# Weights in 2 MB transfers into pairs of pieces: a two-layer hybrid with two mixture-of-experts stages

## The chip, the cores and the metric

The kernel runs on one core of one Trainium2 chip (trn2). A core has TensorE (PE), VectorE (DVE), ScalarE (ACT), GpSimd (POOL) and SyncE (SP), which only issues transfers here, and 16 DMA engines. The metric is the time of one execution on the device in microseconds (us), the median of several. Memory of the chip is called HBM, the working memory of a core has 128 partitions.

## The reference

Two layers over x of 256 tokens x 1024 features, in fp32:

```
u = rms_norm(h); h = h + mixer(u); u = rms_norm(h); h = h + moe(u)

mixer of layer 0: proj = u @ w_in (1024 x 3592), split into seven parts of 512 and one of 8;
    a gated recurrence over chunks (8 heads of 64), and causal attention with a forget gate
    (8 heads of 64); both joined, @ w_out (1024 x 1024)
mixer of layer 1: q, k, v = u @ w_in (1024 x 3072); q, k normalised by head, their gains, rope;
    8 heads, each softmax(q1 k1) - lam * softmax(q2 k2), times v; normalised, @ w_out
moe: 4 groups of 8 experts; each token takes the best group, and its best 2 experts in it;
    for g: y += (silu(x @ w_gate[g]) * (x @ w_up[g]) * combine) @ w_down[g]
    w_gate, w_up: 1024 x 512 and w_down: 512 x 1024 for each of 32 experts
```

The weights of one expert are three matrices of 2 MB (1 MB here is 1024 KB), 192 MB a layer; the mixers have 17 matrices of 2 MB. All of it is read once: 418 MB in 1 MB pieces of 128 partitions x 2048 numbers.

## The kernel before

**Stages.** Mixer 0, experts of layer 0, mixer 1, experts of layer 1. In a mixer the tokens' features are turned by PE and split into two float parts (`transposed`), each weight piece is split too into a high and a low part (`Weights.ahead`: ACT copies at L294, DVE subtracts at L295), and each product is three matmuls (`mm3`, L269 to L271). In an expert stage the tokens are sorted to experts, up to 32 tokens (CAP) an expert, eight rounds (`qd`) of four experts (`es`). An expert takes 16 products with gate and up (L1254, two matmuls each on the chip), SiLU and product on ACT and DVE, 16 products with down (L1264). The first expert's products with gate and up stand apart (`first_products`, L1199), so do the last expert's (`products` L1295, `down` L1306), whose results are scattered back to the tokens (L1226) and added to h (L1232).

**The ring.** `Slots` is a ring `R` of 22 slots of 1 MB (128 x 2048 numbers). It is both the place where weight pieces land and the place of the mixers' work buffers: `alloc` and `hold` give a slot to the program, `free(n, keep)` gives slots back, of which `keep` stay reserved for later buffers, and `want(n)` keeps back the next ones given free. Whatever is not live and not reserved is filled by `pump` with the next piece in the order of use: one transfer of 1 MB (L102), 8192 contiguous bytes a partition. The split weights take slots too, `SPLIT` of them at a time, one for each half of a piece.

**What sets the order.** The transfers stand in one queue, issued by SP in program order. Each one waits for its slot (the last engine that used it), and on one of eight semaphore lanes (DMAHW0 to 7 in the order), that is for the landing of the transfer eight before it; a transfer that waits holds up all behind it. The order of work on the engines is made by a scheduler from the program's order, the data and the free tiles, with some edges written by hand (`issue_after`). PE's products of the projections are spread by it between the heads' steps: scores (L375), turning probabilities (L402), applying them (L410 to L414), turning a head's result (L861).

**Other transfers** on the queue: x, constants, `wrt` (the router's weights of a layer, 160 KB, L214; the second layer's go out after the last reader of the first's, L999 on PE) and the output.

Of the kernel before, what the change touches and what calls it, by code (L numbers as in the profile page):

```python
# [29 lines left out]
SLOTS = 22  # L30
SPLIT = (5, 5)
KEPT = 5 + SPLIT[0], 3 + SPLIT[1]

# [11 lines left out]
V_FQ, V_FK, V_DQ, V_DK, V_N = 70, 71, 72, 136, 200  # L45
# [14 lines left out]
class Slots:  # L60


    def __init__(self, nc, pool, chunks, n, reserve):
        self.nc, self.pool, self.chunks, self.n = nc, pool, chunks, n
        self.live, self.reserve, self.due = 0, reserve, 0
        self.issued, self.taken = [], 0

    def tile(self, dt=F32):
        return self.pool.tile([P, 2048], dt, name="w", tag="w", bufs=self.n)

    def alloc(self, dt=F32):
        assert self.reserve > 0
        self.reserve -= 1
        self.live += 1
        return self.tile(dt)

    def hold(self):

        t = self.alloc()
        self.nc.gpsimd.memset(t[:, 0:1], 0.0)  # L80
        return t

    def halves(self):
        t = self.hold()
        return t[:, 0:1024], t[:, 1024:2048]
# [11 lines left out]

    def pump(self, most=1000):
        while most > 0 and self.live + self.reserve < self.n and len(self.issued) < len(self.chunks):
            src, k = self.chunks[len(self.issued)]  # L100
            w = self.tile().rearrange("p (k f) -> p k f", k=k)
            self.nc.sync.dma_start(out=w, in_=src)  # L102
            self.issued.append(w)
            self.live += 1
            most -= 1

    def take(self):
        self.taken += 1
        return self.issued[self.taken - 1]

# [12 lines left out]
def hybrid_kernel(ctx: ExitStack, tc: tile.TileContext, x, pos, vec, wr, wbf, const,  # L123
# [4 lines left out]
    ring = ctx.enter_context(tc.tile_pool(name="ring", bufs=SLOTS))  # L128
# [38 lines left out]
    wbh = cst.tile([P, 2, KD, 8], F32R, name="wbh")  # L167
# [16 lines left out]
    def pieces(w, ks):  # L184

        return [(w[i].rearrange("p (k f) -> p k f", k=k), k) for i, k in enumerate(ks)]
# [16 lines left out]
    chunks = pieces(w_mix0, KS0) + experts(0) + pieces(w_mix1, KS1) + experts(1)  # L203
    R = Slots(nc, ring, chunks, SLOTS, KEPT[0])
    R.pump(2)
    nc.sync.dma_start(out=ct[:, C_N0:C_N], in_=const[:, C_N0:C_N])
    nc.sync.dma_start(out=wbt, in_=wbf)
    R.pump(2)
# [17 lines left out]
    def transposed(gain, W=None):  # L226

        uh, ul = (R.alloc(F32R).rearrange("p (k s) -> p k s", k=KD) for _ in range(2))

# [43 lines left out]
    class Weights:  # L273


        def __init__(self, n, slots):
            self.n, self.free = n, slots
            self.ready, self.rest = [], []

        def ahead(self, most=1000):  # L280
            while self.n > 0 and self.free > 0 and most > 0:
                most -= 1
                self.n -= 1
                self.free -= 1
                last = len(self.rest) == 1
                if not last:
                    w = R.take()
                    k = w.shape[1]
                    self.rest = [w[:, :, i * P:i * P + P] if k == KD else w[:, i * k // 2:(i + 1) * k // 2, :]
                                 for i in range(2)]  # L290
                w = self.rest.pop(0)
                t = R.alloc(F32R)
                hi, lo = (t[:, 1024 * i:1024 * i + 1024].rearrange("p (k f) -> p k f", k=w.shape[1]) for i in range(2))
                self.split = A.copy(out=hi, in_=w)  # L294
                V.tensor_tensor(out=lo, in0=w, in1=hi.bitcast(F32), op=ALU.subtract)  # L295
                if last:
                    R.free(1)
# [6 lines left out]
        def done(self):  # L304
            self.free += 1
            R.free(1, keep=1 if self.n > 0 else 0)
# [109 lines left out]
    def maps():  # L416


        x = [R.hold() for _ in range(2)]
        Ls = [[x[1][:, 384 * (2 * i + j):384 * (2 * i + j) + 384] for j in range(2)] for i in range(2)]  # L420
        Ls.append([w[:, 1536:1920] for w in x])
        return pairs(x[0]), Ls
# [4 lines left out]
    def split_halves():  # L427

        a = R.alloc(F32R)
        return tuple(a[:, 1024 * i:1024 * i + 1024].rearrange("p (m t) -> p m t", m=4) for i in range(2))  # L430

    class OutProj:
# [18 lines left out]
        def first(self, o):  # L451
            for k in range(4):
                self.block(o, k, k == 0)
            R.free(1)
# [20 lines left out]
    def even():  # L475
        v4 = lambda a: a.rearrange("p (m t) -> p m t", m=4)
        uT, ia, iv = transposed(vt[:, V_GM:V_GM + 8])
        W = Weights(36, SPLIT[0])
# [26 lines left out]
        f_, B_ = R.halves()  # L505
        f, B = v4(f_), v4(B_)
        q2_ = R.hold()
        Az_ = R.hold()
# [7 lines left out]
        R.want(3)  # L516
# [52 lines left out]
        Ts, g_ = R.halves()  # L569
        ST0_, ST1_ = R.halves()  # L570
        STh = [v4(a) for a in (ST0_, ST1_)]
        S1_, va_ = R.halves()
# [73 lines left out]
        R.free(1)  # L646
# [81 lines left out]
        o = []  # L728
        R.want(1)
        R.free(2)  # L730
        values()
        qk = [v4(a) for a in R.halves()]
# [3 lines left out]
        R.want(1)  # L736
        first_out(3)
        R.free(1)
        first_out(1)
        heads_in(qk[1], vt[:, V_FK:V_FK + 1])  # L740
        R.want(1)
        PT, Ls = maps()
        R.free(1)
        R.want(1)
        R.free(1)
        R.want(1)
        o.append(split_halves())
        softmax(0, qk, Ls[0], PT[0])
        PT += pairs(R.hold())
        softmax(1, qk, Ls[1], PT[1])  # L750
        gates(0, *o[0])
        R.want(1)
        softmax(2, qk, Ls[2], PT[2])
        gates(1, *o[0])
        R.free(2)
        softmax(3, qk, Ls[0], PT[3])
        o.append(split_halves())
# [9 lines left out]
        R.free(2)  # L767
        second_out(3, PT[3], *o[1])
        R.free(1, keep=1)
# [4 lines left out]
    def rope_tables():  # L774
# [18 lines left out]
        for i, (off, scale) in enumerate(((V_DQ, 0.125), (V_DK, 1.0))):  # L793
            gv = vt[:, off:off + 64].rearrange("p (a b) -> p a b", a=2).unsqueeze(1).broadcast_to([P, NT, 2, 32])
            for j, tr in enumerate((cos, sin)):
                dst = rope_t[:, 2 * i + j].rearrange("p t (a b) -> p t a b", a=2)
                G.tensor_tensor(out=dst, in0=gv, in1=tr.unsqueeze(2).broadcast_to([P, NT, 2, 32]), op=ALU.mult)
# [3 lines left out]
    def odd(W):  # L801
        uT, ia, _ = transposed(vt[:, V_GM + 8:V_GM + 16], W)
# [23 lines left out]
        qk = [[v4(a) for a in R.halves()]]  # L826
# [51 lines left out]
        o = []  # L878
        R.want(2)
        heads_in(qk[0], 0)  # L880
        qk.append([v4(a) for a in R.halves()])
        o.append(split_halves())
        R.want(1)
        heads_in(qk[0], 1)
        R.want(1)
        PT, Ls = maps()
        R.want(2)
        R.free(1)
        p0 = [soft(0, qk[0], Ls[0]), soft(1, qk[0], Ls[1])]
        heads_in(qk[1], 0)  # L890
        with tc.issue_after(W.last.ins):
            p_transposed(p0, PT[0])
        W.ahead()
        PT += pairs(R.hold())
        v = [a.rearrange("p (t c) -> p t c", t=NT) for a in R.halves()]
# [13 lines left out]
        head_out(3, v[0], PT[1], *o[0])  # L909
        R.free(1)  # L910
        head_out(2, v[0], PT[1], *o[0])
        R.want(1)
        R.free(1)
        o.append(split_halves())
# [3 lines left out]
        R.free(1)  # L918
# [3 lines left out]
        R.free(2)  # L922
        head_out(6, v[1], PT[3], *o[1])
        head_out(7, v[1], PT[3], *o[1])
        R.free(1, keep=1)
# [6 lines left out]
    def moe(l, op):  # L932
        gain = vt[:, V_GF + 8 * l:V_GF + 8 * l + 8]
        hk = h.rearrange("p t (q k) -> p t k q", k=KD)
        work = [R.alloc()]
# [252 lines left out]
        def first_products():  # L1188
# [7 lines left out]
            for n in range(2):  # L1196
                for x_ in range(2):
# [3 lines left out]
                    R.free(1)  # L1201
# [34 lines left out]
        spare = 0  # L1236
        for qd in range(8):
# [5 lines left out]
            if qd == 7 and l == 0:  # L1243
                spare = KEPT[1] - 8
            ys = buffers(qd)[1]
            for es in range(4 if qd < 7 else 3):
                if qd == 0 and es == 0:
                    hid = hidden(*gp0)
                else:
# [6 lines left out]
                    R.free(4, keep=min(spare, 4))  # L1256
                    spare -= min(spare, 4)
# [12 lines left out]
                R.free(2, keep=1 if qd == 0 and es == 0 else 0)  # L1270
# [9 lines left out]
                if es == 2 and qd == 0:  # L1280
                    work.append(R.alloc())
# [158 lines left out]
```

## Time and profile before

| what | value |
|---|---|
| median of 3 runs | 1208.14 us (1207.39 to 1208.32) |
| profiled execution: time, span | 1205.45 us, 1203.8 us |
| mean granted clock of TensorE | 0.937 |
| busy: PE, DVE, ACT, POOL | 1021.5, 351.1, 297.0, 54.1 us (85, 29, 25, 4%) |
| weights' queue | 441.44 MB, its packets 89.7% of the 16 engines' span |
| mean rate over the span | 368 GB/s |

The span is from the first to the last instruction; the execution's time has 1.65 us more around it. Busy times are sums over engines that work side by side, so what ends a stage is read from the waits in that stage, not from these shares. A packet is one contiguous run of a transfer on one DMA engine.

### The profile page before, as it was taken

What the parts mean: (1) busy time and instruction counts of PE and PEld (TensorE: products, weight loads), DVE (VectorE), ACT (ScalarE), POOL (GpSimd) and SP (SyncE); (2) the same over time, 40 slices, a digit from 0 to 9 for tenths busy, and PEclk for the clock granted to TensorE, in tenths of its full rate; (3) what the DMA queues carried; (4) which work ended last, traced back from release to release, by engine and by line L of the source; (5) the groups of instructions that cost most, each with busy time, mean ns of one, the idle gap of its engine ahead of it and who ended that gap; (6) DMA issues with size and microseconds to landing.
All of it is one profiled execution on the core that took longest, in us unless ns stands there. A gap on an engine that the chain in (4) does not pass through costs nothing.

```text
span 1203.8 us, 17689 instructions
## 1 busy us (share of the span) xinstructions
PE 1021.5 (85%) x7284; PEld 589.9 (49%) x7284; DVE 351.1 (29%) x879; ACT 297.0 (25%) x681; POOL 54.1 (4%) x100
## 2 busy tenths in 40 slices
PE   7999998898887878787788999888787868786877
PEld 7878774353433434233256778455352424252523
DVE  7877633011111101001068876311111111110101
ACT  7266532111111111101164575211111111111111
POOL 2130001000000000000002100000000000000000
PEclk8999988889989899889999999999998998998898
DMA  9741969999999999999995369799999999999996
GB/s 374 320 141 42 356 268 421 421 421 420 420 421 418 420 421 421 421 421 421 416 419 198 105 210 363 288 419 420 421 421 421 421 420 420 421 420 420 421 422 273
DMA packets 63685, 442.62 MB, mean 368 GB/s; under 512 B 7152, under 2 KB 7664, under 8 KB 10608
## 3 DMA queue, kind: packets, MB, share of 16 engines
q1 hardware_dynamic: 63600, 441.44, 89.7%
q8 instruction: 59, 0.97, 0.3%
q14 instruction: 26, 0.21, 0.0%
HBM read 440.37 MB, written 1.05 MB: 367 GB/s over the span
## 4 chain that ended last, share of the span: by engine, by line
DMA 45%; PE 18%; DVE 3%; ACT 2%; issue 1%; POOL 0%; SPq 0%; ACTq 0%; DVEq 0%; POOLq 0%
DMA w<-w_up 17%; DMA w<-w_gate 15%; DMA w<-w_down 13%; PE pa L1254 3%; PE pa L270 2%; PE pa L271 2%; PE pa L269 2%; PE pb L1077 1%; PE pa L1264 1%; PE pc L375 1%; PE pc L1226 1%; PE pb L1112 1%; PE pa L1226 1%; DVE w L295 1%; PE pb L1179 1%
## 5 line engine op out<-in xcount | busy, mean ns | idle before, releaser
L1254 PE MATMUL pa<-w 128*32 128x512 f32 x1920 | 307.3, 648 | 64.0 <-DMA w<-w_up 55.1
L1254 PEld LDWEIGHTS pa<-w 128*32 128x32 f32 x1920 | 72.1, 118 | 263.4 <-issue 140.4
L1264 PE MATMUL pa<-w,hid 128*32 128x256 f32 x1984 | 142.2, 432 | 34.6 <-DVE hid L1115 34.6
L1115 DVE TENSOR_TENSOR hid<-hid,pb 128x128 f32<-128x128 f32 x64 | 18.4, 288 | 485.8 <-ACT hid L1114 485.8
L1109 ACT COPY s<-pa 128x512 f32<-128x512 f32 x68 | 39.8, 585 | 403.7 <-PE pa L1254 360.4
L269 PE MATMUL pa<-w 128*128 128x512 f32 (+1 forms) x320 | 120.9, 379 | 3.3 <-ACT w L294 3.3
L270 PE MATMUL pa<-w 128*128 128x512 f32 (+1 forms) x320 | 118.8, 371 | 1.4 <-DVE w L295 1.4
L271 PE MATMUL pa<-w 128*128 128x512 f32 (+1 forms) x320 | 118.3, 370 | 1.8 <-DVE w L295 1.8
L1112 PEld LDWEIGHTS pb<-ct,s 128*128 128x128 f32 x544 | 66.0, 191 | 104.6 <-ACT s L1109 102.6
L1077 PE MATMUL pb<-s,h 128*128 128x128 f32 x448 | 115.8, 409 | 0.0
L1112 PE MATMUL pb<-ct,s 128*128 128x64 f32 (+1 forms) x544 | 74.2, 280 | 47.3 <-ACT s L1109 47.3
L1077 PEld LDWEIGHTS pb<-s,h 128*128 128x128 f32 x448 | 109.5, 334 | 9.3 <-issue 9.3
L1268 DVE COPY w<-pa 32x256 f32<-32x256 f32 x124 | 52.4, 423 | 179.5 <-ACT w L1268 179.1
L1264 PEld LDWEIGHTS pa<-w,hid 128*32 128x32 f32 x1984 | 63.3, 120 | 83.8 <-DVE hid L1115 41.3
L1268 ACT COPY w<-pa 32x256 f32<-32x256 f32 x124 | 44.9, 362 | 233.3 <-PE pa L1264 190.8
L295 DVE TENSOR_TENSOR w<-w 128x1024 fp32r<-128x1024 f32 x68 | 86.6, 1285 | 8.9 <-ACT w L294 8.6
L294 ACT CAST w<-w 128x1024 fp32r<-128x1024 f32 x68 | 70.0, 1046 | 22.1 <-PE pa L271 11.5
L269 PEld LDWEIGHTS pa<-w 128*128 128x128 f32 x320 | 61.7, 193 | 14.3 <-ACT w L294 4.1
L270 PEld LDWEIGHTS pa<-w 128*128 128x128 f32 x320 | 61.8, 193 | 12.4 <-issue 2.5
L271 PEld LDWEIGHTS pa<-w 128*128 128x128 f32 x320 | 61.6, 192 | 11.2 <-DVE w L295 2.1
L1096 POOL TENSOR_TENSOR s<-OH,CW 128x128 f32<-128x128 f32 x36 | 14.6, 406 | 830.8 <-PE pb L1112 518.3
L1226 PE MATMUL pc<-w,s 128*128 128x512 f32 (+1 forms) x64 | 36.7, 656 | 9.5 <-DVE w L1268 9.3
(264 smaller groups left out, 754.6 us busy)
## 6 DMA issues: line engine op xcount, KB each, us to landing
w<-w_gate SPq DMA_DIRECT2D x128, 1024.0 KB, 19.8
w<-w_up SPq DMA_DIRECT2D x128, 1024.0 KB, 19.8
w<-w_down SPq DMA_DIRECT2D x128, 1024.0 KB, 19.8
w<-w_mix SPq DMA_DIRECT2D x34, 1024.0 KB, 17.8
h<-x SPq DMA_DIRECT2D x2, 512.0 KB, 4.2
out<-h SPq DMA_DIRECT2D x4, 256.0 KB, 2.0
ct<-const SPq DMA_DIRECT2D x1, 468.0 KB, 9.8
wrt<-wr SPq DMA_DIRECT2D x2, 160.0 KB, 9.6
```

The lines of the kernel that those rows point to most:

```text
L269: T.matmul(out=out, lhsT=lhsT[0], rhs=rhs[0], start=start, stop=False)
L270: T.matmul(out=out, lhsT=lhsT[0], rhs=rhs[1], start=False, stop=False)
L271: return T.matmul(out=out, lhsT=lhsT[1], rhs=rhs[0], start=False, stop=stop)
L294: self.split = A.copy(out=hi, in_=w)
L295: V.tensor_tensor(out=lo, in0=w, in1=hi.bitcast(F32), op=ALU.subtract)
L1077: T.matmul(out=pt[:, k, :], lhsT=hk[:, t, 4 * n + k, :], rhs=og[:, t, :], start=t == 0, stop=t == NT - 1)
L1109: A.copy(out=gs, in_=g.rearrange("p (f k) -> p k f", k=4))
L1112: T.matmul(out=tp[:, k, c], lhsT=gs[:, k, :], rhs=r, start=True, stop=True)
L1226: m = T.matmul(out=y[t][:, n, :], lhsT=Sm[:, t * P:(t + 1) * P], rhs=ys, start=start, stop=stop)
L1254: T.matmul(out=gp[32 * j:32 * j + 32, :], lhsT=xg[:, 4 * (j % 2) + kk, 32 * es:32 * es + 32], rhs=w[j][:, kk, :], start=kk == 0, stop=kk = ...
L1264: m = T.matmul(out=dp[32 * j:32 * j + 32, :], lhsT=hid[:, k, :], rhs=w[k // 2][:, k % 2, 256 * j:256 * j + 256], start=k == 0, stop=k == 3 ...
L1268: (V.tensor_copy if j % 2 else A.copy)(out=ys[32 * es:32 * es + 32, 256 * j:256 * j + 256], in_=dp[32 * j:32 * j + 32, :])
```

## The change

Weights come in units of 2 MB, a whole matrix: one transfer of 16384 contiguous bytes a partition, into a tile of 128 x 4096 that holds two pieces. (The mixers' weights are laid out for that; the first two units of mixer 0 and each layer's last expert still come as two transfers of 1 MB.) The ring has 11 such pairs, room for 24 pieces with two single work buffers beside it; these two take the work buffers that need one slot. `drop(n)` counts pieces that are used up and gives a pair back when both are; split weights have three pairs, six halves, instead of five slots. `first_products` uses gate's two pieces, then up's, where it alternated. Gains of rope come by a transfer of their own (256 KB, in the middle of mixer 0) instead of within `vec`.

```diff
-SLOTS = 22
-SPLIT = (5, 5)
-KEPT = 5 + SPLIT[0], 3 + SPLIT[1]
+PAIRS = 11
+SPLIT = 3
+KEPT = 2 + SPLIT, 1 + SPLIT
+SCRATCH = 1024
...
-        return self.pool.tile([P, 2048], dt, name="w", tag="w", bufs=self.n)
+        return self.pool.tile([P, 4096], dt, name="w", tag="w", bufs=self.n)
+
+    def single(self):
+        return self.pool.tile([P, 2048], F32, name="o", tag="o", bufs=2)
...
+    def drop(self, n):
+
+        self.dropped += n
+        while self.ends and self.ends[0] <= self.dropped:
+            self.ends.pop(0)
+            self.free()
+
     def pump(self, most=1000):
-        while most > 0 and self.live + self.reserve < self.n and len(self.issued) < len(self.chunks):
-            src, k = self.chunks[len(self.issued)]
-            w = self.tile().rearrange("p (k f) -> p k f", k=k)
-            self.nc.sync.dma_start(out=w, in_=src)
-            self.issued.append(w)
+        while most > 0 and self.live + self.reserve < self.n and self.units:
+            w = self.tile()
+            a = 0
+            for src, k, n in self.units.pop(0):
+                self.nc.sync.dma_start(out=w[:, 2048 * a:2048 * (a + n)].rearrange("p (k f) -> p k f", k=k), in_=src)
+                for _ in range(n):
+                    self.issued.append(w[:, 2048 * a:2048 * a + 2048].rearrange("p (k f) -> p k f", k=k // n))
+                    a += 1
+            self.ends.append(len(self.issued))
...
-            r += [(v[i][:, 4 * a:4 * a + 4, :], 4) for v in (gate_v, up_v) for a in range(2)]
             if e < NE - 1:
-                r += [(down_v[i][:, 2 * a:2 * a + 2, :], 2) for a in range(2)]
+                r += [[(v[i], k, 2)] for v, k in ((gate_v, 8), (up_v, 8), (down_v, 4))]
             else:
-                r += [(down_v[i][:, :, 512 * a:512 * a + 512], 4) for a in range(2)]
+                r += [[(v[i][:, 4 * a:4 * a + 4, :], 4, 1) for a in range(2)] for v in (gate_v, up_v)]
+                r.append([(down_v[i][:, :, 512 * a:512 * a + 512], 4, 1) for a in range(2)])
...
         def done(self):
-            self.free += 1
-            R.free(1, keep=1 if self.n > 0 else 0)
+            self.used += 1
+            if self.used % 2 == 0:
+                self.free += 1
+                R.free(1, keep=1 if self.n > 0 else 0)
...
+        R.free(1)
+        nc.sync.dma_start(out=own, in_=rope)
         softmax(3, qk, Ls[0], PT[3])
...
-            for n in range(2):
-                for x_ in range(2):
+            for x_ in range(2):
+                for n in range(2):
                     for k in range(4):
                         m = T.matmul(out=gp0[x_][32 * k:32 * k + 32, :], lhsT=xg[:, 4 * n + k, 0:CAP],
                                      rhs=w[2 * x_ + n][:, k, :], start=n == 0, stop=n == 1, tile_position=(0, 32 * k))
-                    R.free(1)
+                R.drop(2)
...
-                    R.free(4, keep=min(spare, 4))
-                    spare -= min(spare, 4)
+                    R.drop(4)
```

On SP, at the end of mixer 0, before (w_ are slots of the ring; the slot numbers tell the rows apart):

```order
L102 DMA w_1661<-w_down 128x2048 [waits DMAHW3_49,PE_49]
L102 DMA w_1721<-w_gate 128x2048 [waits DMAHW4_49,PE_49]
L102 DMA w_1723<-w_gate 128x2048 [waits DMAHW5_49,PE_49]
L102 DMA w_1725<-w_up 128x2048 [waits DMAHW6_49,DVE_49]
L214 DMA wrt_71<-wr 128x320 [waits DMAHW7_49,PE_49]
L102 DMA w_1832<-w_up 128x2048 [waits DMAHW0_49,PE_49]
L102 DMA w_1838<-w_down 128x2048 [waits DMAHW1_49,PE_49]
L102 DMA w_1844<-w_down 128x2048 [waits DMAHW2_49,PE_49]
```

and in the same place after:

```order
L112 DMA w_1598<-w_down 128x4096 [waits DMAHW4_49,PE_49]
L112 DMA w_1658<-w_gate 128x4096 [waits DMAHW5_49,DVE_49,PE_49]
L112 DMA w_1660<-w_up 128x4096 [waits DMAHW6_49]
L112 DMA w_1771<-w_down 128x4096 [waits DMAHW7_49,PE_49]
L112 DMA w_1781<-w_gate 128x4096 [waits DMAHW0_49,PE_49]
L112 DMA w_1824<-w_up 128x4096 [waits DMAHW1_49,PE_49]
L236 DMA wrt_71<-wr 128x320 [waits DMAHW2_49]
L112 DMA w_1926<-w_down 128x4096 [waits DMAHW3_49,PE_49]
```

The gate and first up piece of expert 3 (w_1721 to w_1725) are the last before `first_products` in the kernel before, and w_1832, the second up piece, the first after it; now both matrices (w_1658, w_1660) are ahead of it, and w_down of expert 3 (w_1771) is the first that waits for its products. The router's transfer has gone behind three transfers of the expert stage.

On PE, near the end of mixer 1, at the head before the last, before:

```order
L271 MATMUL pa<-w 128x512
L269 MATMUL pa<-w 128x512
L270 MATMUL pa<-w 128x512
L271 MATMUL pa<-w 128x512
L861 MATMUL pb<-s_5298,ct 128x256
L402 MATMUL pc<-ct,w 128x128
```

and after, where L291 to L293 are the product of L269 to L271, L436 is L414, L424 is L402 and L870 is L861:

```order
L436 MATMUL pb<-w 128x128
L291 MATMUL pa<-w 128x512
L292 MATMUL pa<-w 128x512
L424 MATMUL pc<-ct,o 128x128
L870 MATMUL pb<-s_5014,ct 128x256
L424 MATMUL pc<-ct,o 128x128 x2
```

Before, nine product rows stand between this head's last L414 and L861 (its last four are shown), after there are two; behind the last head 36 product rows follow in a row where 21 did.

## Rows read from the trace of the kernel before

**Rows 1.** Slices of the page: busy tenths of PE and of the DMA engines

```profile
PE   7999998898887878787788999888787868786877
DMA  9741969999999999999995369799999999999996
```

**Rows 2.** Chain that ended last, by engine and line (page)

```profile
DMA 45%; PE 18%; DVE 3%; ACT 2%; issue 1%; POOL 0%; SPq 0%; ACTq 0%; DVEq 0%; POOLq 0%
DMA w<-w_up 17%; DMA w<-w_gate 15%; DMA w<-w_down 13%; PE pa L1254 3%; PE pa L270 2%; PE pa L271 2%; PE pa L269 2%; PE pb L1077 1%; PE pa L1264 1%; PE pc L375 1%; PE pc L1226 1%; PE pb L1112 1%; PE pa L1226 1%; DVE w L295 1%; PE pb L1179 1%
```

**Rows 3.** Windows: mixer 0, expert stage 0, mixer 1, expert stage 1

```profile
core 0: us, PE busy (x) PEld busy (x) DVE busy (x) ACT busy (x) POOL busy (x), PEclk, DMA share, GB/s
20.00:160.00 140.00, 138.78 (x1240) 114.31 (x1240) 102.98 (x213) 76.95 (x158) 15.64 (x33) 1.00 0.63 241
...
180.00:606.00 426.00, 350.10 (x2558) 168.86 (x2554) 56.00 (x166) 57.59 (x146) 9.94 (x24) 0.92 1.01 420
...
612.00:750.00 138.00, 129.86 (x636) 99.80 (x634) 110.32 (x271) 85.24 (x199) 16.02 (x16) 0.99 0.65 245
...
770.00:1174.00 404.00, 325.23 (x2390) 158.05 (x2388) 50.86 (x139) 50.53 (x126) 6.91 (x17) 0.94 1.01 421
```

**Rows 4.** Chain of waits from 1134 us: start, us, what

```profile
1134.36 19.82 DMA w<-w_gate
...
1154.24 19.82 DMA w<-w_up
...
1174.11 5.50 PE pa L1254 x26
```

**Rows 5.** DMA from 300 to 400 us: all packets, the weights' queue

```profile
DMA packets 5761, 42.01 MB, mean 420 GB/s; under 512 B 639, under 2 KB 639, under 8 KB 639
...
q1 hardware_dynamic: 5751, 41.88, 100.9%
```

**Rows 6.** DMA from 600.5 to 602.8 us

```profile
DMA packets 384, 0.91 MB, mean 394 GB/s; under 512 B 14, under 2 KB 14, under 8 KB 360
```

**Rows 7.** DMA from 1187 to 1189 us

```profile
DMA packets 340, 0.76 MB, mean 379 GB/s; under 512 B 12, under 2 KB 12, under 8 KB 326
```

**Rows 8.** Queue of instruction fetches: packets, MB, share (page)

```profile
q8 instruction: 59, 0.97, 0.3%
```

**Rows 9.** Timeline of SP at the first expert's products, both layers

```profile
174.23 0.33 SPq L102 DMA_DIRECT2D w<-w_up  x1
175.27 1.19 SPq L102 DMA_DIRECT2D w<-w_down  x2
...
761.72 0.33 SPq L102 DMA_DIRECT2D w<-w_up  x1
762.58 1.19 SPq L102 DMA_DIRECT2D w<-w_down  x2
```

**Rows 10.** DMA issues from 174 to 174.5 us: KB, us to landing

```profile
w<-w_up SPq DMA_DIRECT2D x1, 1024.0 KB, 5.1
```

**Rows 11.** Waits of SP from 160 to 180 us: total, times, longest

```profile
SPq L102 <- PE pa L1199: 14.3, 4, 12.8
```

**Rows 12.** Groups by line (page): the split's two steps

```profile
L295 DVE TENSOR_TENSOR w<-w 128x1024 fp32r<-128x1024 f32 x68 | 86.6, 1285 | 8.9 <-ACT w L294 8.6
L294 ACT CAST w<-w 128x1024 fp32r<-128x1024 f32 x68 | 70.0, 1046 | 22.1 <-PE pa L271 11.5
```

**Rows 13.** Timeline of PE from 728 us: two products in turn

```profile
729.41 0.40 PE L269 MATMUL pa<-w 128*128 128x512 f32 x1
729.64 0.39 PE L270 MATMUL pa<-w 128*128 128x512 f32 x1
```

**Rows 14.** Waits of PE from 612 to 765 us: total, times, longest

```profile
PE pb L363 <- DVE s L837: 4.1, 6, 1.0
```

More of the change, by code (lines that the diff above doesn't have):

```diff
@@ L109, in take, with halves @@
         return self.issued[self.taken - 1]
+def halves(t):
+    return t[:, 0:1024], t[:, 1024:2048]
 class Banks:
@@ L273, in hybrid_kernel, with __init__ @@
     class Weights:
-        def __init__(self, n, slots):
-            self.n, self.free = n, slots
+        def __init__(self, n, pairs):
+            self.n, self.free, self.used = n, pairs, 0
             self.ready, self.rest = [], []
         def ahead(self, most=1000):
-            while self.n > 0 and self.free > 0 and most > 0:
+            while self.n > 0 and most > 0 and (self.rest or self.free > 0):
                 most -= 1
                 self.n -= 1
-                self.free -= 1
-                last = len(self.rest) == 1
-                if not last:
+                if not self.rest:
                     w = R.take()
                     k = w.shape[1]
[L289 to L293, printed above, removed]
+                    self.free -= 1
+                    self.rest = list(zip([w[:, :, i * P:i * P + P] if k == KD else w[:, i * k // 2:(i + 1) * k // 2, :]
+                                          for i in range(2)], R.alloc(F32R)))
+                w, t = self.rest.pop(0)
+                hi, lo = (a.rearrange("p (k f) -> p k f", k=w.shape[1]) for a in halves(t))
                 self.split = A.copy(out=hi, in_=w)
                 V.tensor_tensor(out=lo, in0=w, in1=hi.bitcast(F32), op=ALU.subtract)
-                if last:
-                    R.free(1)
+                if not self.rest:
+                    R.drop(1)
                 self.ready.append((hi, lo))
@@ L427, in split_halves @@
     def split_halves():
-        a = R.alloc(F32R)
-        return tuple(a[:, 1024 * i:1024 * i + 1024].rearrange("p (m t) -> p m t", m=4) for i in range(2))
+        return [[a.rearrange("p (m t) -> p m t", m=4) for a in halves(t)] for t in R.alloc(F32R)]
     class OutProj:
@@ L567, in even @@
         V.tensor_tensor(out=nc2[32:40], in0=ncum, in1=nc2[0:8].bitcast(F32), op=ALU.subtract)
[L569 to L572, printed above, removed]
+        Tg, ST_ = R.hold()
+        Ts, g_ = halves(Tg)
+        STh = [v4(a) for a in halves(ST_)]
+        S1_, va_ = halves(R.single())
         ST1 = S1_.rearrange("p (a m t) -> p a m t", a=2, m=4)
@@ L725, in heads_in @@
                 transpose_heads(head_norm(pt, t), dst, t, gain)
-        o = []
-        R.want(1)
-        R.free(2)
+        R.free(1, keep=1)
         values()
-        qk = [v4(a) for a in R.halves()]
+        qk_, x1 = R.hold()
+        qk = [v4(a) for a in halves(qk_)]
+        R.want(2)
         heads_in(qk[0], gq)
@@ L825, in odd @@
         v4 = lambda a: a.rearrange("p (m t) -> p m t", m=4)
-        qk = [[v4(a) for a in R.halves()]]
+        qk = [[v4(a) for a in halves(R.single())]]
         def rope(pt, i, t):
@@ L875, in values @@
                 A.mul(out=v[:, t, :], in_=pt, mul=rsm[:, t:t + 1])
-        o = []
+        heads_in(qk[0], 0)
+        qk_, x0 = R.hold()
+        qk.append([v4(a) for a in halves(qk_)])
         R.want(2)
[L880 to L883, printed above, removed]
         heads_in(qk[0], 1)
[L885 to L888, printed above, removed]
+        o = split_halves()
+        Ls = maps((x0, R.single()))
         p0 = [soft(0, qk[0], Ls[0]), soft(1, qk[0], Ls[1])]
         heads_in(qk[1], 0)
+        PT = pairs(x0)
         with tc.issue_after(W.last.ins):
@@ L893, in odd @@
         W.ahead()
-        PT += pairs(R.hold())
-        v = [a.rearrange("p (t c) -> p t c", t=NT) for a in R.halves()]
+        x2, v_ = R.hold()
+        PT += pairs(x2)
+        v = [a.rearrange("p (t c) -> p t c", t=NT) for a in halves(v_)]
         heads_in(qk[1], 1)
@@ L1269, in moe @@
                                                          in_=dp[32 * j:32 * j + 32, :])
-                R.free(2, keep=1 if qd == 0 and es == 0 else 0)
+                if (l, qd, es) == (0, 7, 2):
+                    R.want(KEPT[1])
+                R.drop(2)
                 if qd == 0 and es == 0:
@@ L1331, in moe @@
                 finish_y(n)
-        R.free(2, keep=2 if l == 0 else 0)
         if l == 0:
@@ L1408, in mix @@
     def mix(*parts):
-        return np.stack([a.reshape(P, 2048) for part in parts for a in part])
+        v = np.stack([a.reshape(P, 2048) for part in parts for a in part])
+        return v.reshape(-1, 2, P, 2048).transpose(0, 2, 1, 3)
     arrays = {
```

114 lines of the change are left out of this document (47 added, 67 removed).

## The prediction

> **What bounds the kernel now.** I read the slices first: the DMA digits stand at 9 wherever experts are worked on, and fall to 1 in two places, the two mixers, where the PE digits are highest [rows 1]. Then the chain of waits, to see which of the two sets the end: 45% of the span is transfers of expert weights, 18% PE [rows 2]. The windows by stage say it stage by stage [rows 3]: in both expert stages the DMA share is 1.01 at 420 and 421 GB/s and PE is busy 350.1 of 426 and 325.2 of 404 us; in the mixers PE is busy 138.8 of 140 and 129.9 of 138 us, at 241 and 245 GB/s. So a mixer costs what PE takes for it, and an expert stage what the transfers take. In the expert stages the chain goes from transfer to transfer in steps of 19.82 us [rows 4]. A transfer waits for the landing of the one eight before it (the waits on the DMA lanes in the order of SP), so 1 MB takes 19.82 / 8 = 2.478 us. After the last big w_up has landed at 1174.06, PE is on the chain until the end: 29.7 us that no transfer rate changes.
>
> Only three things can move the time: the rate in the expert stages, how many pieces are in the ring when a mixer gives way to its expert stage, and PE's path through the mixers.
>
> **The rate.** Between 300 and 400 us the weights' queue moves 5751 packets; 639 are under 512 bytes (the semaphore writes at a transfer's end), so 5112 are of 8 KB [rows 5]: 16 engines x 100 us / 5112 = 313.0 ns each. Runs of 16384 bytes make it one packet where two were. What a packet costs besides its bytes is in the windows in which 2 KB runs move (the last w_down of a layer). From 600.5 to 602.8: 384 packets, 346 of 2 KB and 24 of 8 KB, so (16 x 2300 - 24 x 313) / 346 = 84.6 ns [rows 6]. From 1187 to 1189: 314 and 14, so (32000 - 14 x 313) / 314 = 87.9 ns [rows 7]. A straight line through 2 and 8 KB gives a fixed part of 84.6 - (313.0 - 84.6) / 3 = 8.5 ns, or 87.9 - (313.0 - 87.9) / 3 = 12.9 ns. I take 8.5, since the queue is full there on both sides; the second window lies in the tail. It is 1.4% of two packets (626 ns). A 2 MB transfer is 128 packets, 8 an engine, and saves 8 x 8.5 = 68 ns. In each layer 192 pieces are needed, 22 are there before the stretch begins and the last 6 keep 1 MB: 164 pieces or 82 transfers, 5.6 us a layer, 11.2 us in both. With 12.9 ns it is 17 us.
>
> The line is carried from 8 to 16 KB, where no load of the trace lies. From below, the nearest row is that of instruction fetches: 59 packets of 16.4 KB in 0.3% of 16 engines' span (57.8 us), about 0.98 us each against the line's 0.62 [rows 8]. They go elsewhere and come singly, so I don't take their number, but they keep the end open on which a long packet gains nothing.
>
> The Trainium skill has a rule for the size of this term ("DMA: Bandwidth & Descriptors", Why small descriptors are slow): about 3 cycles of overhead a descriptor beside one cycle per 32 bytes. By it 2 KB would run (67/64) / (259/256) = 3.5% slower a byte than 8 KB, and doubling 8 KB would give 0.58%. The trace shows 8% and 12% for the first (4 x 84.6 and 4 x 87.9 against 313), two to three times the rule, so I keep the line; by the rule the term would be 4.7 us instead of 11.2.
>
> **The room.** Each expert stage begins with the 16 products of expert 0 (L1199), and before them SP stands still, at the longest 12.8 us in the first layer [rows 11]: the ring is full, 21 pieces of experts in it. At 174.23 the first slot is free and the next transfer goes out [rows 9]; it lands 5.1 us later [rows 10], and each MB after it 2.478 later. So the 22nd, 23rd and 24th expert piece are there at 179.35, 181.8 and 184.3. In the new order the ring holds 11 pairs, all 22 pieces, and the next transfer (w_down of expert 3) waits for the eighth product, where before's second issue went out: 175.27. Landing: 175.27 + (5.1 - 2.48) + 2 x 2.444 = 182.8, with 24 pieces instead of the 184.3 of before: 1.5 us earlier. Against it, the 160 KB of the router's second layer, which before landed in the idle time behind w_up, now come behind these transfers: 160/1024 x 2.478 = 0.39 us. Net 1.1 us. In the second layer the same from 761.72 and 762.58: 24 pieces at 771.8 before, at 770.1 after, 1.7 us. Both are hidden only if the pairs are full by then. Pairs come free later than single slots, since both halves must be used. Two more pieces are 5 us of DMA; SP's 12.8 us there leave 7.8 us for lateness. That covers it in my reading of the waits: in the new order the last pairs before that place (w_gate and w_up of expert 3) wait for the same last part of the mixer as the last pieces did.
>
> Does the ring stall later? 8 transfers of 2 MB can be out and PE holds two pairs while it works on gate and up, one on down: 11. Before it was 8 of 22 slots. A pair that PE gives back late then stalls the queue, but a queue with 7 transfers out has 34 us of work, and PE is idle for 18% of the stage [rows 3], so it gives pairs back in time. I cost it at nothing; without that cover SP would wait for L1254 and the transfers would run dry, 2.5 us for each MB that goes out late.
>
> **The mixers.** Same matmuls, another order, as the scheduler makes it from the freed tiles. PE has 1.2 us of idle time in mixer 0 and 8.1 in mixer 1; half of the latter waits on DVE in the heads (L363: 4.1 us in 6 waits) [rows 3, 14]. At the end of the odd mixer, the order puts two products of the output projection between the last part of one head and the turn of its result (L861, now L870), where there were nine; 15 products more are left behind the last heads. A product of 512 columns is issued every 0.23 us [rows 13], so 15 x 0.23 = 3.4 us of cover has moved behind the place where it could hide DVE. The last head before had three products there and PE lost nothing, so some of it was not needed. I take +2.5 us for both mixers. Bounds: all idle time gone, 1.2 + 8.1 = -9.3; as much again, +9.3.
>
> The other edits cost nothing that I can find. The 256 KB of rope gains (0.6 us of DMA) go through while the queue idles in mixer 0; SP stands at them until the second gates are done, and the transfer behind them needs a later part of the mixer anyhow. The loop over x_ before n changes no count. The two single work buffers replace slots of the ring that were held at the same times. The last expert's transfers and the tail are as they were.
>
> **Sum.** -11.2 - 1.1 - 1.7 + 2.5 = -11.5 us. The profiled execution took 1205.45 us (span 1203.8 us and 1.6 around it), the median of the runs shown is 1208.14, 2.7 more; I carry the difference over: 1208.14 - 11.5 = 1196.6 us, -0.95%. Its own range: the rate term from half of 11.2 (a line that bends) to 17, the mixers from -3 to +6; not all ends meet, so 1188 to 1204.
>
> **Rivals.**
> *A long packet is no faster.* What costs 8.5 ns would belong to each 2 KB run as a row of memory or a burst, not to the packet. For it: no 16 KB load in the trace, and the fetches of rows 8. Against it: a byte in 2 KB runs costs 8 to 12% more than in 8 KB runs [rows 5 to 7], so something is paid by the run, and 8 KB is no size at which it would have to end. Then -1.1 - 1.7 + 2.5 = -0.3: 1207.8 us, no change. The Trainium skill's rule that 512 bytes suffice for the line rate (same page, Specifications) is on this side; the 379 and 394 GB/s of 2 KB runs against 420 speak against it.
>
> *The tail's window is right.* 12.9 ns a packet, 17 us in both layers, the rest as forecast: 1208.14 - 17 - 2.8 + 2.5 = 1190.8 us. The stretch is as full as the other; that it is the tail, with a PE that holds nothing up, makes it the less like the expert stages.
>
> *PE starves in the mixers.* The split weights had five single slots and have three pairs, and a pair is given back only when both halves are used. Place: the products of the projections, which wait on L294 or L295. The split of a half takes 1.05 us on ACT and then 1.29 on DVE [rows 12]; if PE uses up a pair and the next can't be split before a pair is free, it stands for 2.3 us. There are 34 pairs in both mixers. From five stalls the 11.5 us are eaten; ten give 23 - 11.5 = +11.5: 1219.6 us. Against it: 24 products of 0.23 us keep PE busy for 5.5 us a half, 11 us a pair, while splitting two halves takes 3.6, with two other pairs ready.
>
> **Chances.** Forecast 0.55; no faster packet 0.17; the tail's window 0.16; starving PE 0.12. A change of 0.2%, 2.4 us, is about what a measurement here can tell from none. The forecast is faster but for 0.02 within the bound, the tail's window faster. The packet that is no faster leaves the mixers to decide: 0.04 faster, 0.08 same, 0.05 slower. Starved cases: 0.04 faster, 0.02 same, 0.06 slower. Together 0.77, 0.12, 0.11. The range 1187 to 1209 takes in no change and the first slower cases; outside are most starved cases and gains over 21 us.
>
> **What would show it.** Landings of 2 MB 4.89 us apart, 39.1 us from issue to landing with eight out (2 x 19.82 less 1.4%), 426 GB/s between 300 and 400 us, packets of 16 KB of about 617 ns. The stretch from L1199's products to the stage's last w_down shorter by 6.5 to 7.5 us in each layer. The first 2 MB after the products issued one product-group later than now, landing 7.5 us later. The wait on L1199 still several us long. PE's idle time in mixer 1 some 10 us, with no waits on L294 or L295 that return with each pair. The forecast is wrong if the rate stays at 420 (then the packet is not what costs) or if the mixers grow by over 6 us.

## The result, and the profile after

The changed kernel takes 1190.18 us, median of 4 runs (1188.60 to 1191.75), the kernel before in the same call 1207.77 us (1207.10 to 1208.32): ratio 0.9855, 95% interval 0.9838 to 0.9872, 17.6 us faster. The forecast was 11.5 us less and 1196.6 us, with a range from 1188 to 1204 at its sum and one from 1187 to 1209 at its chances; the measured time lies in both, near their lower ends. A later call gave 1189.41 against 1206.15 us, ratio 0.9859 (0.9842 to 0.9876). The profiled executions took 1188.60 and 1205.45 us, a difference of 16.85, spans 1187.0 and 1203.8 us.

The slices after, which answer to [rows 1]: the DMA digits are as high in the expert stages, and the gaps lie in the mixers as before.

```profile
PE   7999998888877877786788999888887868786867
DMA  9702989999999999999993348899999999999996
```

The windows by stage after, columns as in [rows 3]. The expert stages run at 426 and 427 GB/s where they had 420 and 421; 100% of the DMA engines as before.

```profile
20.00:160.00 140.00, 138.94 (x1250) 114.66 (x1249) 103.30 (x217) 76.51 (x160) 10.74 (x22) 1.00 0.58 233
180.00:597.00 417.00, 331.86 (x2538) 166.11 (x2534) 54.71 (x158) 56.64 (x139) 10.57 (x25) 0.91 1.01 426
612.00:750.00 138.00, 130.36 (x640) 101.36 (x639) 101.03 (x270) 76.61 (x189) 13.20 (x10) 0.98 0.59 235
762.00:1158.00 396.00, 315.44 (x2396) 157.60 (x2388) 51.16 (x141) 50.90 (x127) 6.86 (x17) 0.90 1.01 427
```

The span can be cut at four places that both traces have: the first expert's products (L1199, now L1201) and the last addition to h (L1232, now L1234) of each layer. Before, from the timeline of PE and the chain of waits (start, duration):

```profile
172.24 4.67 PE L1199 MATMUL pa<-w 128*32 128x512 f32 x32
...
611.69 0.69 DVE h L1232
...
759.76 4.46 PE L1199 MATMUL pa<-w 128*32 128x512 f32 x32
...
1199.57 0.69 DVE h L1232
```

and after:

```profile
171.19 3.64 PE L1201 MATMUL pa<-w,o 128*32 128x512 f32 x32
...
602.59 0.69 DVE h L1234
...
752.07 3.64 PE L1201 MATMUL pa<-w,o 128*32 128x512 f32 x32
...
1183.24 0.69 DVE h L1234
```

| stage | before | after | difference | forecast |
|---|---|---|---|---|
| start, mixer 0, to the products | 172.24 | 171.19 | -1.05 | mixers together +2.5 |
| products to the last addition, layer 0 | 439.45 | 431.40 | -8.05 | -5.6 - 1.1 |
| mixer 1, to the products | 148.07 | 149.48 | +1.41 | (above) |
| products to the last addition, layer 1 | 439.81 | 431.17 | -8.64 | -5.6 - 1.7 |
| rest of the span | 4.23 | 3.76 | -0.47 | 0 |

The expert stages give 16.7 us of the 16.8, the mixers next to nothing. How much of 16.7 is rate and how much is room is seen from the landings in the traces. From the landing of the 24th expert piece to that of the last w_down it is 168 pieces: 184.32 to 606.73 and 771.82 to 1194.23 before, 422.4 us both times; 180.96 to 597.54 and 761.92 to 1178.08 after, 416.6 and 416.2 us. So the rate gave 5.8 and 6.2 us, and 0.42 us of the first went to the router's transfer, which now lies in this stretch. The remainder, 2.2 and 2.4 us, lies at the start of the stages: the 24th piece lands 12.1 us after the products began before, and 9.8 and 9.9 us after.

### The profile page after: what moved, and what is told of

Its sections match the earlier page's. It is cut to its first block, busy times and chain, and to the rows that moved or that the text cites. A ratio compares the mean times of both kernels' runs of the same rounds, so it can differ in the third digit from the quotient of the medians.

```text
span 1187.0 us, 17235 instructions
## 1 busy us (share of the span) xinstructions
PE 993.0 (84%) x7284; PEld 586.6 (49%) x7284; DVE 348.3 (29%) x879; ACT 296.3 (25%) x681; POOL 52.0 (4%) x90
## 3 DMA queue, kind: packets, MB, share of 16 engines
HBM read 440.56 MB, written 1.05 MB: 372 GB/s over the span
## 4 chain that ended last, share of the span: by engine, by line
DMA 46%; PE 43%; DVE 5%; ACT 4%; issue 2%; POOL 1%; SPq 0%; ACTq 0%; DVEq 0%; POOLq 0%
DMA w<-w_up 20%; DMA w<-w_down 16%; DMA w<-w_gate 10%; PE pa L1253 8%; PE pa L1262 5%; PE pa L293 4%; PE pa L291 4%; PE pa L292 4%; PE pb L1079 4%; PE pb L1114 2%; PE pc L1228 2%; DVE w L315 1%; PE pb L1181 1%; PE pa L1228 1%; ACT s L1111 1%
## 5 line engine op out<-in xcount | busy, mean ns | idle before, releaser
L1253 PE MATMUL pa<-w,o 128*32 128x512 f32 x1920 | 278.4, 673 | 76.5 <-DMA w<-w_up 65.2
L1253 PEld LDWEIGHTS pa<-w,o 128*32 128x32 f32 x1920 | 68.1, 121 | 254.4 <-issue 159.1
L291 PE MATMUL pa<-w 128*128 128x512 f32 (+1 forms) x320 | 119.6, 375 | 3.3 <-ACT w L314 3.3
L293 PE MATMUL pa<-w 128*128 128x512 f32 (+1 forms) x320 | 118.3, 372 | 1.8 <-DVE w L315 1.8
L1266 DVE COPY o<-pa 32x256 f32<-32x256 f32 x124 | 52.4, 423 | 201.8 <-ACT o L1266 201.2
L1266 ACT COPY o<-pa 32x256 f32<-32x256 f32 x124 | 44.9, 362 | 210.2 <-PE pa L1262 178.2
L315 DVE TENSOR_TENSOR w<-w 128x1024 fp32r<-128x1024 f32 x68 | 85.0, 1272 | 9.8 <-ACT w L314 9.6
L314 ACT CAST w<-w 128x1024 fp32r<-128x1024 f32 x68 | 68.5, 1045 | 22.1 <-PE pa L293 16.8
L291 PEld LDWEIGHTS pa<-w 128*128 128x128 f32 x320 | 61.7, 193 | 14.2 <-ACT w L314 3.8
L293 PEld LDWEIGHTS pa<-w 128*128 128x128 f32 x320 | 61.7, 193 | 12.1 <-DVE w L315 2.1
L1228 PE MATMUL pc<-o,s 128*128 128x512 f32 (+1 forms) x64 | 38.8, 691 | 11.1 <-DVE o L1266 11.1
## 6 DMA issues: line engine op xcount, KB each, us to landing
w<-w_gate SPq DMA_DIRECT2D x62, 2048.0 KB, 39.1
w<-w_up SPq DMA_DIRECT2D x62, 2048.0 KB, 39.1
w<-w_down SPq DMA_DIRECT2D x62, 2048.0 KB, 39.1
```

The costliest lines, as they stand in the source:

```text
L291: T.matmul(out=out, lhsT=lhsT[0], rhs=rhs[0], start=start, stop=False)
L293: return T.matmul(out=out, lhsT=lhsT[1], rhs=rhs[0], start=False, stop=stop)
L1228: m = T.matmul(out=y[t][:, n, :], lhsT=Sm[:, t * P:(t + 1) * P], rhs=ys, start=start, stop=stop)
L1253: T.matmul(out=gp[32 * j:32 * j + 32, :], lhsT=xg[:, 4 * (j % 2) + kk, 32 * es:32 * es + 32], rhs=w[j][:, kk, :], start=kk == 0, stop=kk = ...
L1266: (V.tensor_copy if j % 2 else A.copy)(out=ys[32 * es:32 * es + 32, 256 * j:256 * j + 256], in_=dp[32 * j:32 * j + 32, :])
```

## The experiments

All times are medians; each ratio is against the kernel before on the same chip (1206.1 to 1206.9 us there). Where two experiments are compared with each other, or with the 1190.2 us above, they ran on different chips: the changed kernel itself gave 1190.2 and 1189.4 us on two.

**1. Two transfers of 1 MB into each pair.** Nothing else of the change is undone.

```diff
-                r += [[(v[i], k, 2)] for v, k in ((gate_v, 8), (up_v, 8), (down_v, 4))]
+                r += [[(v[i][:, k // 2 * a:k // 2 * a + k // 2, :], k // 2, 1) for a in range(2)]
+                      for v, k in ((gate_v, 8), (up_v, 8), (down_v, 4))]
...
-    units = pieces(w_mix0, KS0, 4) + experts(0) + pieces(w_mix1, KS1, 0) + experts(1)
+    units = pieces(w_mix0, KS0, 100) + experts(0) + pieces(w_mix1, KS1, 100) + experts(1)
```

> The changed kernel with every pair filled by two transfers of 1 MB (8192 contiguous bytes a partition); ring, pairs and order of frees stay. Theory (the length of a packet is most of the gain): the expert stages go back to 2.478 us a MB, 420 GB/s, and last about 6.2 us longer each: 1190.2 + 12.5 = 1202.7 us. Rival (the gain is the ring's room and the way pairs come free): the rate of the transfers doesn't matter to it, 1190 to 1192 us.

1201.93 us, ratio 0.9956 (0.9939 to 0.9972). The rival is out: 11.8 us of the gain go when the transfers are halved, with ring and frees as changed. What is left against before, 4.6 us, is not rate. By the traces 1.6 and 2.4 us of it are room: the 24th piece lands 10.5 and 9.6 us after the products began, where before it was 12.1 us. The DMA view from 300 to 400 us reads as in [rows 5] again:

```profile
DMA packets 5761, 42.02 MB, mean 420 GB/s; under 512 B 637, under 2 KB 637, under 8 KB 637
```

**2. One transfer of 2 MB in 8 KB packets.** A gap of 16 bytes between the halves of a pair (the expectation says 32) breaks each run in two where it lands; the source stays 16384 contiguous bytes a partition, and the number of transfers and of semaphore writes stays. SCRATCH is halved to make room.

```diff
-        return self.pool.tile([P, 4096], dt, name="w", tag="w", bufs=self.n)
+        return self.pool.tile([P, 4104], dt, name="w", tag="w", bufs=self.n)
...
+                if n == 2:
+                    d = w.rearrange("p (a f) -> p a f", a=2)[:, :, 0:2048]
+                    src = src.rearrange("p (a k) f -> p a (k f)", a=2)
```

> The changed kernel with a gap of 32 bytes between the two halves of a pair, so that a transfer of 2 MB consists of 8 KB packets; number of transfers, lanes and semaphore writes as changed. Theory (the packet's length): as the kernel with two transfers of 1 MB but for one semaphore write of 9 ns a pair, 1201 us. Rival (the number of transfers, their issue and their semaphore writes cost the time, not the packets): 1190 us.

1203.89 us, ratio 0.9978 (0.9969 to 0.9988). The DMA view from 300 to 400 us, first of this kernel:

```profile
DMA packets 5448, 42.05 MB, mean 421 GB/s; under 512 B 320, under 2 KB 320, under 8 KB 320
```

then of the changed kernel:

```profile
DMA packets 2928, 42.71 MB, mean 427 GB/s; under 512 B 320, under 2 KB 320, under 8 KB 320
```

Both have 320 semaphore writes, 20 transfers of 2 MB, and the rate is 421 and 427 GB/s. From the 24th piece to the last w_down it takes 422.5 and 422.1 us, as before the change. So it is the packet's length, not the number of transfers, and not the length of the run in HBM, which is as in the change. One thing more differs than was meant: SP is busy with one issue for 4.6 us (median from 300 to 400 us; 0.33 in the changed kernel), and mostly seven transfers are out, not eight, as the page's row of landings shows (32.7 us at 4.97 us a transfer; 39.1 us in the changed kernel):

```profile
w<-w_up SPq DMA_DIRECT2D x62, 2048.0 KB, 32.7
```

Whether that comes of the 256 packets of a transfer or of the halved SCRATCH is not shown. It does not explain the rate, since the weights' packets fill 100.8% of the 16 engines' time in this window, 100.3% in the changed kernel. That this kernel is 2 us above the first was not expected: its stages have the same rate, but its first restart comes 3.15 us after the products began (2.57 in the first), as TensorE's granted clock is 0.50 from 168 to 172 us and 0.54 from 172 to 174 (0.85 in the first), and its mixers took 0.1 and 0.4 us more.

**3. Short runs.** Two transfers of 1 MB as in 1, pieces interleaved by rows:

```diff
+                if mixed:
+                    v = w.rearrange("p (k a f) -> p a k f", a=2, k=k)[:, a]
```

> As the kernel with two transfers of 1 MB, but the pieces of an expert's pair are interleaved in it by rows: gate and up land in runs of 2 KB, down in runs of 4 KB. With a fixed part of 8.5 ns a packet a MB costs 24 x 8.5 = 204 ns more in 2 KB runs and 68 ns more in 4 KB runs, 0.95 us an expert, some 52 us in all: 1255 us. With 12.9 ns (the tail's window) 79 us: 1282 us. With about 3.5 ns, three cycles, 21 us: 1224 us. A straight line wants the landings of gate, up and down at 2.68, 2.68 and 2.55 us a MB (8.5 ns).

1257.58 us, ratio 1.0422 (1.0404 to 1.0439), 55.7 us above experiment 1: the line with 8.5 ns said 52, the tail's window 79. In the full queue the trace has the landings of gate and up 2.69 to 2.72 us a MB apart, those of down 2.56 to 2.58 (2.48 in 8 KB runs): (2.70 - 2.48) / 24 = 9 ns and (2.57 - 2.48) / 8 = 11 ns a packet. From 8 to 16 KB it is (2 x 2.48 - 4.89) / 8 = 9 ns. From 2 to 16 KB one line fits, with 9 to 11 ns a packet; SP's issues are slow here too (2.6 us, median), and the packets fill 103% of the engines' time. The Trainium skill's fixed overhead of some 3 cycles a packet ("DMA: Bandwidth & Descriptors", Why small descriptors are slow) would be a third of that by the recorded estimate of 3.5 ns, and the measurement decides against it here.

**4. The first products in the old order.**

```diff
-            for x_ in range(2):
-                for n in range(2):
+            for n in range(2):
+                for x_ in range(2):
...
-                R.drop(2)
+            R.drop(4)
```

> The changed kernel with the first expert's products in the old order (gate and up in turn), so that the gate pair is free after 12 of 16 products instead of 8 and the up pair after 16. Theory (the products ran twice as fast at the first 8 because TensorE's granted clock was 1.0 there and 0.5 before, the order has no part in it): the first transfer goes out 0.9 us later in each layer, +1.7 us: 1192 us, and products 0.43 us apart as now. Rival (the order made them faster): products take 1 us more as well, +3.8 us: 1194 us.

1191.35 us, ratio 0.9874 (0.9858 to 0.9891): near the theory's number, but the interval overlaps that of the changed kernel, so the timeline has to decide. In layer 0 the products keep their pace, and by SP's timeline the first transfer goes out 173.52 - 170.68 = 2.84 us after the first product instead of 1.98, a step of four products later:

```profile
173.52 0.33 SPq L112 DMA_DIRECT2D w<-w_down  x1
174.38 0.33 SPq L112 DMA_DIRECT2D w<-w_gate  x1
```

In layer 1 it is 3.15 us, since the first products ran at the lower clock there (longest matmul 922 ns, 617 in layer 0). The order has no part in the faster products of layer 0; the new order frees the gate pair 0.9 us earlier there. The 1.2 us of layer 1 hold the lower clock too.

**5. Ten pairs.**

```diff
-PAIRS = 11
+PAIRS = 10
```

> The changed kernel with 10 pairs instead of 11. Theory (room counts by the piece: the queue is idle from the moment the ring is full until the first expert's products free a pair): two pieces less are there at either restart, 4.89 us a layer, 1190.2 + 9.8 = 1200 us, with the rate as changed, 427 GB/s between 300 and 400 us. Rival (the pairs before that place come free so late that the last one is not loaded in time anyway; in the changed kernel the last landing is 0.7 and 2.8 us ahead of the next issue): little is lost, 1190 to 1194 us.

1201.19 us, ratio 0.9953 (0.9936 to 0.9969). 11 us more than with 11 pairs; the rate is 426 GB/s as with 11. The stages last 437.84 and 437.90 us, 6.4 and 6.7 more: 4.89 for two pieces that are not there, 0.4 since the restart lags 2.4 us behind the products here, and about 1 in which PE ends the stage later after the last w_down. The rival is out. The lag of 2.4 us is TensorE's clock: the trace has the same matmuls in the same order as the changed kernel up to the products of either layer, and yet a granted clock of 0.50 from 170 to 172 us, where the changed kernel has 0.73 (longest matmul of the products 1019 and 999 ns; 617 and 618 in the changed kernel).

**6. Two and four pairs for split weights.**

```diff
-SPLIT = 3
+SPLIT = 2
```

> The changed kernel with 2 pairs for split weights instead of 3. Theory (PE takes 11 us for a pair and splitting two halves 3.6 us, so three pairs are not short): mixers within 3 us of those of the changed kernel, 1187 to 1193 us. Rival (pairs given back only whole starve PE; 2.3 us a stall, 34 pairs): with 2 pairs a stall at most pairs, +40 us or more, and then the 1.5 us by which mixer 1 has grown are the first of these stalls.

1205.13 us, ratio 0.9990 (0.9980 to 0.9999). A miss for both: 15 us lost, more than the theory had and less than the rival; 14 of them in mixer 0, which ends at 185.18 instead of 171.19, while mixer 1 takes 150.77 us. With 2 pairs PE is idle in the middle of mixer 0, here from 110 to 140 us with two pairs:

```profile
110.00:140.00 30.00, 24.71 (x106) 16.24 (x104) 20.37 (x77) 15.82 (x48) 0.00 (x0) 0.89 0.58 208
```

and with three:

```profile
110.00:140.00 30.00, 29.94 (x158) 22.76 (x158) 22.99 (x73) 20.72 (x55) 0.00 (x0) 1.00 0.91 359
```

PE does 106 instead of 158 matmuls there. From 20 us to the products it is idle for 10.9 us instead of 3.0. Of these 8 us more, 3.6 are waits for the split's own lines (2.4 on L314, 1.2 on L315, both in the window above), which the changed kernel has none of in that stretch. The other 6 us by which mixer 0 grew are busy time; the mean granted clock is 0.96 instead of 0.98. That with less split ahead the scheduler has fewer products to put between the steps of the heads would explain the rest of the idle time, but is not shown. So starving PE is a real mechanism one pair below the change.

> The changed kernel with 4 pairs for split weights instead of 3. Theory (the growth of mixer 1 from 148.1 to 149.5 us is the order of products among the heads, not a shortage of split weights): mixer 1 stays at 149 to 150 us; less prefetch in the mixers costs up to 5 us at a restart, 1190 to 1200 us. Rival (split weights are short with 3 pairs): mixer 1 falls back to 148 us or less.

1191.86 us, ratio 0.9877 (0.9859 to 0.9895). Mixer 1 takes 149.26 us. More split pairs don't bring it back to 148 us; with three they were not short. The price came in mixer 0, which ends at 174.58, 3.4 us later, and not at a restart: the products run to the last additions in 432.3 and 431.6 us, within 1 us of the changed kernel.

**7. Repeats, and 21 slots in the kernel before.**

> The changed kernel once more, beside the kernel before, as the measure for the runs above, which were timed against 1206.5 to 1206.7 us of before. Theory: 1189 to 1191 us; the first expert's products take 0.43 us a step from the start in layer 1 again, since TensorE's clock is back at 1.0 there; in layer 0 that may differ by a step or two, and a restart that lags 2.0 to 3.0 us instead of 1.98 would mean that about 1 us of the gain hangs on when the clock rises. Rival: both restarts lag 1.98 us again, and the earlier clock belongs to the changed order of work.

1189.41 us. Products at 170.73 and 751.40 us, both restarts 1.98 us behind them, mixer 1 149.35 us. The rival's first half holds: the earlier clock at this place comes back. Its second half, that it belongs to the changed order of work, does not: the ten pairs of experiment 5 have the same order and the lower clock.

> The kernel before once more, for a second profile of it. Theory (mixer 0 shorter by 1 us and mixer 1 longer by 1.4 us belong to the changed order of work, not to one execution): first expert's products start at 172.2 us, 148.1 us from the end of the first expert stage to the products of the second, a restart that lags 2.0 us behind four products at the lower clock in both layers. Rival (they are scatter of single executions, the clock's above all): products at 171.2, 149.5 us, lags of 1.1 us.

A single run, 1205.23 us. Products at 172.56 us, mixer 1 147.77 us, and at both places products at the lower clock (longest matmul 1062 and 1059 ns, where the changed kernel has 618 at most). So mixer 0's gain and mixer 1's loss belong to the two kernels. The clock at the products came back in both as well, but by experiment 5 it is not fixed by the order of work.

```diff
-SLOTS = 22
+SLOTS = 21
```

> The kernel before with 21 slots instead of 22. Theory (each piece of room is worth the time of one piece at each restart): 2.48 us a layer, 1206.5 + 5 = 1211.5 us. Rival (room only counts where it makes the difference between landed and not landed before the products): less than 2 us in all.

1210.80 us, ratio 1.0035 (1.0022 to 1.0048): 3.9 us for one piece in each layer, near the theory's 5; the two stages last 2.3 and 1.9 us more. The price of room is about the same in the old ring: one slot less puts the landing of the 24th piece 2.6 us further behind the products, one pair less in the new ring 5.5 and 5.7 us. Not tested is the other direction: pairs and single buffers together hold 24 pieces, where the kernel before had 22 slots. What the kernel before would gain from that much room is not known, so the part of the gain that is room is not shown to need transfers of 2 MB.

## Why the prediction was right, and where it was off

**The sum.** By the profiled executions the change gave 16.8 us where 11.5 were forecast, and every term was off to the same side: the rate by 1.3 us, the room by 1.4, the mixers by 2.1 and the rest of the span, for which there was no term, by 0.5.

**The rate: right.** 5.6 us a layer were forecast, 6.2 and 6.2 measured (without the router's transfer in the first). From the products to the last w_down the layers are 8.1 and 8.5 us shorter, more than the 6.5 to 7.5 given as a sign of the forecast. Issue to landing is 39.1 us with eight out, as forecast, and the chain's steps are such transfers now. The row of the DMA issues after (KB each, us to landing):

```profile
w<-w_up SPq DMA_DIRECT2D x62, 2048.0 KB, 39.1
```

and the last step of the chain of waits:

```profile
1119.05 38.94 DMA w<-w_up
...
1158.03 5.07 PE pa L1253 x28
```

The line from 2 and 8 KB packets held at 16 KB; 9 to 10 ns would have been the better fixed part than 8.5. The rival that a long packet is no faster is refuted by experiments 1 and 2.

**The room: mechanism right, a term mis-sized.** Forecast net 1.1 and 1.7 us, measured 1.8 (2.2 less the 0.4 of the router's transfer) and 2.4. I let the first transfer go out where the eighth product ended before, 1 us after the fourth. In the changed kernel eight products take as long as four did: SP's issue, the first row of its timeline there, is 1.98 us after the first product; before it was 174.23, 1.99 us after it [rows 9].

```profile
173.17 0.33 SPq L112 DMA_DIRECT2D w<-w_down  x1
174.89 0.33 SPq L112 DMA_DIRECT2D w<-w_gate  x1
```

The windows show why. Before, around the products:

```profile
170.00:172.00 2.00, 2.00 (x10) 0.50 0.00 0
172.00:174.00 2.00, 2.00 (x14) 0.50 0.05 12
174.00:176.00 2.00, 2.00 (x24) 0.91 0.43 86
```

After (PE busy, granted clock, DMA share, GB/s):

```profile
168.00:170.00 2.00, 2.00 (x10) 0.50 0.94 401
170.00:172.00 2.00, 2.00 (x14) 0.73 0.44 180
172.00:174.00 2.00, 2.00 (x24) 1.00 0.00 0
```

The granted clock is 0.50 (1.2 GHz) until 174 us before, and 1.00 (2.4 GHz) again from about 171 us after; in both it fell at 164 us, after PE had been idle for 0.7 and 1.0 of the 2 us from 160 to 162. By that clock the first transfer went out 1.0 and 0.8 us earlier than forecast, a step that the prediction did not have; the landing took 0.3 us of that back (7.8 us after the issue, where the sum had 7.5). Why the clock rises 3 us earlier is open: the loop's order is not the cause (experiment 4), nor the order of the matmuls ahead (experiment 5), though both kernels repeat their own.

**The cover by SP's wait: right in the sum, wrong as read.** I took SP's wait of 12.8 us before the products [rows 11] as time left for late pairs, 7.8 us of it after two more pieces. After, SP waits even longer there:

```profile
SPq L112 <- PE pa L1201: 17.9, 2, 16.5
```

but the window from 160 to 170 us has its DMA engines busy throughout, at 426 GB/s, where the same ten microseconds before had 238:

```profile
160.00:170.00 10.00, 8.03 (x35) 7.82 (x35) 3.61 (x20) 0.00 (x0) 0.00 (x0) 0.71 1.00 426
```

SP's wait starts when the last transfer is issued, not when it has landed. The last pair, issued at 156.12, landed at 172.51, 0.66 us ahead of the next issue at 173.17 (6.6 before), and 2.75 us ahead of it in layer 1. The engines themselves moved nothing from 172 to 174 us (the last of the windows above), and nothing from 752 to 754 in layer 1, since the first packets of the next transfer come about 1 us after its issue. So the pairs came in time, in layer 0 with 0.66 us to spare by the landing and some 2 us at the engines, and not 7.8. That the ring would not stall later held: the DMA share is 1.01 through both expert stages.

**The mixers: too dear.** +2.5 us forecast, +0.4 measured, as -1.05 and +1.41 (the repeats: -1.8 and +1.6). In mixer 1 the place was right, since the waits of PE on the heads' steps grew. They answer to [rows 14] so (603 to 752 us, all of mixer 1):

```profile
PE pb L385 <- DVE s L846: 4.5, 6, 1.3
...
PE pb L385 <- DVE sm L416: 0.6, 1, 0.6
...
PE pc L424 <- DVE o L856: 0.3, 1, 0.3
```

4.1 became 5.4 us: 1.3 of the 1.4; the other waits of PE there are as before. If the 15 products that moved behind the last heads are the cause, which no run tests, two fifths of their 3.4 us of cover had been needed. Mixer 0 I had at nothing; it lost 0.9 us of PE's busy time (149.06 to 148.17 from 20 us to the products), with the clock that came back earlier.

**The rivals.** The time, 1190.2, is that of the rival with the tail's window, 1190.8, and yet its mechanism is wrong: 12.9 ns a packet would have given 17 us of rate and 79 in experiment 3, and 12 and 56 were measured. Room and mixers made up what it had too much in rate. Starving PE did not occur with three pairs, as forecast; the 14 us of mixer 0 with two say that its chance, 12%, was not set too high.

## What to carry to other kernels

Where a stage runs at the full rate of the DMA queue, the length of the contiguous run is a term of its own: a packet's fixed part, read from any stretch in which shorter runs move, times the packets saved. Room before a stage that waits for transfers was worth about the time of one piece for each piece (by the landings 2.6 us for a slot in the old ring, 5.6 us for a pair in the new), and a wait of the issuing engine is not idle time of the DMA: look at the landings, or at the DMA share of that window. A time that agrees does not show the mechanism; a run that changes one factor does.

## What was not expected of the hardware

A packet's fixed part of 9 to 11 ns is the same from 2 to 16 KB, at 313 ns for 8 KB; twice the semaphore writes made 0.1 and 0.2 us in 422 (experiment 1 against 2: 422.6 against 422.5 us for 168 pieces in layer 0, 422.3 against 422.1 in layer 1). A transfer of 2 MB in 256 packets kept SP at its issue for 4.6 us where one of 128 took 0.33, and the engines stayed full all the same (experiment 2). TensorE's granted clock at the first products of layer 0 was 0.50 in both executions of the kernel before and 1.00 in both of the changed kernel; with ten pairs it was 0.50 as they began, with the same matmuls ahead of them in the same order.
